# Two 512-column units in the input projection of an encoder layer, in place of four of 256

## The chip, the cores and the metric

The kernel runs on one core of a Trainium2 chip. The metric is the device time of one execution in microseconds (us); several executions are timed and their median is given. A profile of one execution shows what each engine did: TensorE (PE in the profile, with its weight loads as PEld), VectorE (DVE), ScalarE (ACT), GpSimd (POOL) and SyncE (SP), whose queue issues nearly all DMA transfers.

## The reference

One encoder layer with one set of weights is applied to 1024 prompt tokens and 256 sample tokens (1280 in all; attention does not cross between the two groups). Everything is float32, the model width is 1024.

```python
n = _rms_norm(h, g_mix, NORM_EPS)
z = jnp.einsum('bsd,dc->bsc', n, w_in).astype(f32)      # w_in: 1024 x 2304
# columns: A queries 512, A keys 512, A values 512, B queries 512, B keys 128, B values 128
qa, ka, va, qb, kb, vb = jnp.split(z, cuts, axis=-1)
...
oa = _diff_attention(qa, ka, va, lam, _alibi_slopes())  # mixer A: 4 heads, two softmax maps each
oa = _rms_norm(oa, g_subln, SUBLN_EPS) * (1.0 - lam_init)
...
qb = _rms_norm(qb.reshape(bsz, s_len, B_HEADS, HEAD_DIM), g_qnorm, NORM_EPS)   # mixer B: 8 query heads
kb = _rms_norm(kb.reshape(bsz, s_len, B_KV_HEADS, HEAD_DIM), g_knorm, NORM_EPS)
qb = _axial_rope(qb, ang_r, ang_c).reshape(bsz, s_len, B_KV_HEADS, B_GROUP, HEAD_DIM)
kb = _axial_rope(kb, ang_r, ang_c)
ob = _gqa_attention(qb, kb, vb).reshape(bsz, s_len, B_WIDTH)
h = h + jnp.einsum('bsc,cd->bsd', jnp.concatenate([oa, ob], axis=-1), w_out)
a = jax.nn.relu(jnp.einsum('bsd,df->bsf', _rms_norm(h, g_mlp, NORM_EPS), w_ff1))
h = h + jnp.einsum('bsf,fd->bsd', a * a, w_ff2)
gate = jax.nn.sigmoid(jnp.einsum('bsd,de->bse', _rms_norm(h, g_ple, NORM_EPS), w_ple_gate))
h = h + gate * jnp.einsum('bsp,pd->bsd', p_l, w_ple_proj)
return _rms_norm(h, g_final, NORM_EPS)
```

## The kernel before

**Numbers.** A float32 operand is split into a high part (rounded to the matmul's input format F32R) and a low part, the rest. A product is three matmuls: high x high, high x low, low x high. `load_w` (L162) does this for weights: a DMA into a staging buffer `raw`, a copy on ScalarE to the high part `wh` (L175), a subtraction to the low part `wl` (L176) on VectorE, or on GpSimd for the narrow A units. `load_x` (L247) does it for x, scaled by the gain, and fills `xh` and `xl`, which stay in SBUF.

**The in-projection.** Tokens come in 10 tiles of 128. Eight blocks of 128 model channels times three products make 24 matmuls for a tile and a unit of columns (`tok_pairs` L264, `mm_gen` L237). The units of columns are:

- `b_unit(2)`: mixer B's keys and values, 256 columns; `va_unit(0)`: values of A's heads 0 and 1, 256 columns. They run in alternation while x is still being loaded: `hook` starts the loads of x and of its row statistics (`stats_x` L256) for the later tokens.
- `b_unit(0)`: four of mixer B's query heads, 256 columns, woven with `va_unit(1)`, values of A's heads 2 and 3.
- `b_unit(1)`: the other four query heads, woven with `qk_a(0)`: keys, then queries of A's head 0, here with the weights stationary and up to 512 tokens as columns (`qk_unit` L372).

`weave` (L214) lets a side generator emit matmuls in proportion to the estimated time of the main one. The weights of the 256-column units share one ring of `WHB` = 11 buffers (each for high and low) and `RAWB` = 6 staging buffers. `load` (L90) chains the input DMAs, so that they are issued in the order of the program on the SP queue.

A `b_unit` tile is followed by `norm_rope` (L278): squares of the psum bank on ScalarE (L283), a scaled copy (L284), the sum per head (L287), a reciprocal root in small operations (L135 to 149), the rotation on GpSimd and VectorE (L292 to 299), and the product with the root (L301). Two tiles later TensorE transposes the result pair of heads by pair (L323). When a chunk of up to 512 tokens is transposed, `finish` (L311) splits it into high and low parts and stores it to DRAM (`qd`, `kd`). A `va_unit` tile is scaled, split (L367, L368) and stored (`vad`, L370). `R` (L444) holds the row statistics of all tokens, transposed by a TensorE instruction into `rp` (L439) and spread over the partitions by way of DRAM; `qk_unit` needs it in L382.

**Attention** reads keys, queries and values back from DRAM. Its rounds are planned by hand: each unit's scores, maxima, exponentials, transposes and value products are put into numbered rounds, and a side generator fills in the A heads 1 to 3 of the in-projection (`qk_rest`), then the output projection. Before round 0 it runs filler of an estimated 14 us (`PRE`). Its tiles take the SBUF that the in-projection's pool `bp` gives back; only two slots, `Q0` and `Q1`, exist from the start, and hold the first keys and queries of mixer B.

The order within each engine comes from a scheduler that simulates the program in time when it is built: among instructions that are ready in that simulation the earlier one in the program goes first, so matmuls of a later tile can stand ahead of those of an earlier one. That order is then fixed. PSUM has eight banks: two for `pj` (`psv`, `psa`), two for `pb` (`psb`), two each for the transposes `tr0` and `tr1` (B's key and value unit also uses `tr1` for two tiles).

The main loop of the first stage and the weave of the others:

```python
gens = [b_unit(2, w_kv, hook), va_unit(0, w_va0)]
for n in range(NT // 2):
    for g in gens:
        for _ in itertools.islice(g, 8):
            pass
...
weave(b_unit(0, w_b0), va_unit(1, w_va1), 1.0)
weave(b_unit(1, wload(1792, dma=load)), qk_a(0), 1.0)
```

## Time and profile before

| what | value |
| --- | --- |
| median of 3 runs | 1715.35 us (1713.63 to 1719.48) |
| the profiled execution | 1713.47 us, span 1711.7 us, granted TensorE clock 0.996 |
| TensorE busy | 1669.0 us, 98% of the span |
| VectorE, ScalarE, GpSimd busy | 69%, 50%, 40% |
| in-projection, up to the last query matmul | to about 183 us |
| first attention scores | 197.4 us |

The span is the part of an execution that the profile shows. Matmuls overlap, so a matmul's own duration is longer than the distance between two of them; the distance is what they cost. "Idle before" is the time for which an engine had nothing, and the name behind the arrow is what ended it.

### The profile page before, as it was taken

The page shows a single profiled execution, that of the slowest core. Times are in us where ns is not written, and L with a number is a line of the kernel's source. Part 1 is how long each engine was busy: PE and PEld are TensorE (multiplying, and loading weights), DVE is VectorE, ACT ScalarE, POOL GpSimd, SP SyncE. Part 2 cuts the span into 40 slices and gives each one's busy share as a digit, 9 for nine tenths or more (in the row PEclk, how much of TensorE's full clock was granted, in tenths as well). Part 3 has the DMA queues.
Part 4 walks back from the last instruction along what each step waited for, and adds up shares of the span by engine and source line. Part 5 has one row for each costly group of instructions (what it writes and reads, how often), then busy time and mean ns, then how long its engine had stood idle before and what let it go on. Part 6 is the DMA issues. An engine that isn't in the chain of part 4 may idle for free.

```text
span 1711.7 us, 27194 instructions
## 1 busy us (share of the span) xinstructions
PE 1669.0 (98%) x9849; PEld 1488.7 (87%) x9849; DVE 1182.8 (69%) x2110; ACT 861.9 (50%) x1731; POOL 691.6 (40%) x671
## 2 busy tenths in 40 slices
...
GB/s 314 271 90 115 202 169 124 141 88 105 273 155 113 165 81 111 150 219 103 158 154 121 132 144 136 128 213 360 198 217 200 129 206 192 167 120 67 35 44 50
DMA packets 187835, 263.60 MB, mean 154 GB/s; under 512 B 13226, under 2 KB 120628, under 8 KB 187700
## 3 DMA queue, kind: packets, MB, share of 16 engines
...
## 4 chain that ended last, share of the span: by engine, by line
PE 81%; DVE 6%; DMA 4%; ACT 3%; issue 3%; POOL 2%; SPq 1%; POOLq 0%; DVEq 0%; ACTq 0%
PE psa L240 6%; PE sc L573 5%; PE pso L240 5%; PE av L651 5%; PE psg L156 4%; PE tr L627 4%; PE psb L240 3%; PE psv L240 2%; DMA xt<-in_x 1%; PE psp L156 1%; DVE pl L638 1%; PE f__14851 L156 1%; PE f__16240 L156 1%; PE f__15200 L156 1%; PE f__16582 L156 1%
## 5 line engine op out<-in xcount | busy, mean ns | idle before, releaser
L1299 ACT ACTIVATE ao<-ar 128x1280 fp32r<-128x1280 f32 x56 | 71.3, 1275 | 193.9 <-PE f__16244 L156 37.9
L573 PE MATMUL sc<-kt,qt 128*128 128x512 f32 (+1 forms) x576 | 156.8, 392 | 7.1 <-ACT p L598 4.7
L638 DVE TENSOR_TENSOR pl<-tr,ph 128x512 fp32r<-128x512 f32 x204 | 137.9, 684 | 32.3 <-ACT ph L633 30.9
L1301 DVE TENSOR_TENSOR ao<-ar,ao 128x1280 fp32r<-128x1280 f32 x56 | 87.7, 1567 | 100.3 <-ACT ao L1299 100.3
L633 ACT ACTIVATE ph<-tr 128x512 fp32r<-128x512 f32 x204 | 119.8, 596 | 57.6 <-PE tr L627 51.2
L1012 POOL TENSOR_SCALAR w1r<-w1r,gmlp 128x256 f32<-128x256 f32 x128 | 98.8, 790 | 68.2 <-DMA w1r<-in_w_ff 45.8
L240 PE MATMUL pso<-ow,mt 128*128 128x512 f32 x480 | 119.6, 395 | 2.9 <-DVE osq L678 1.3
L627 PE MATMUL tr<-ident,p 128*128 128x128 f32 x768 | 116.0, 274 | 6.4 <-DVE pl L638 5.7
L573 PEld LDWEIGHTS sc<-kt,qt 128*128 128x128 f32 x576 | 99.3, 189 | 25.2 <-ACT p L598 6.3
L156 PE MATMUL psg<-gw,n 128*128 128x512 f32 (+1 forms) x504 | 115.4, 384 | 0.0
L627 PEld LDWEIGHTS tr<-ident,p 128*128 128x128 f32 x768 | 91.7, 141 | 23.1 <-DVE pl L638 9.3
L156 PEld LDWEIGHTS psg<-gw,n 128*128 128x128 f32 x504 | 90.8, 188 | 19.5
L1087 ACT ACTIVATE w<-w1s 128x512 fp32r<-128x512 f32 x64 | 40.0, 628 | 133.5 <-POOL w1s L1094 64.2
L240 PEld LDWEIGHTS pso<-ow,mt 128*128 128x128 f32 x480 | 87.6, 189 | 20.9 <-DVE osq L678 2.0
L651 PE MATMUL av<-ph,vt 128*128 128x256 f32 x544 | 102.4, 289 | 1.0 <-DVE osq L678 0.4
L612 POOL TENSOR_SCALAR p<-p,rl 128x1024 f32<-128x1024 f32 x64 | 75.2, 1176 | 50.5 <-DVE rl L610 45.4
L590 DVE TENSOR_REDUCE mm<-sc 128x1 f32<-128x1024 f32 (+1 forms) x80 | 84.2, 1055 | 9.5 <-PE sc L573 9.1
L651 PE MATMUL av<-pl,vt 128*128 128x256 f32 x408 | 89.9, 302 | 0.0
L651 PEld LDWEIGHTS av<-ph,vt 128*128 128x128 f32 x544 | 82.3, 190 | 6.5 <-ACT ph L633 0.9
L598 ACT ACTIVATE p<-sc,mm 128x1024 f32<-128x1024 f32 x64 | 71.3, 1115 | 24.8 <-DVE mm L590 18.5
L586 DVE CUSTOM_DVE_ANT_0 p<-sc,dist 128x1024 f32<-128x1024 f32 x64 | 77.6, 1218 | 8.0 <-PE sc L573 4.4
L595 ACT ACTIVATE p<-p,mm 128x1024 f32<-128x1024 f32 x64 | 73.5, 1149 | 18.4 <-DVE mm L586 17.6
...
## 6 DMA issues: line engine op xcount, KB each, us to landing
...
```

The costliest lines, as they stand in the source:

```text
L156: PE.matmul(ps, a, b, start=start and i == 0, stop=stop and i == n - 1)
L240: PE.matmul(ps, a, b, start=i == 0, stop=i == n - 1)
L573: PE.matmul(ps[:, h0:h0 + n], shared["q"][:, cc, v, i * P:(i + 1) * P], kt[:, s0 + h0:s0 + h0 + n], start=v == 0, stop=v == 1)
L586: V.tensor_tensor_reduce(out=p[:, :sn], in0=ps[:, :sn], in1=dst_t[:, off:off + sn], scale=SLOPES[idx], scalar=3.0e38, op0=ALU.add, op1=ALU ...
L590: V.tensor_reduce(out=st["m", i][:, 0:1], in_=ps[:, :sn], axis=AX.X, op=ALU.max, negate=True)
L612: G.tensor_scalar(p[:, :sn], p[:, :sn], rl[:, 0:1], 1.0, op0=ALU.mult, op1=ALU.mult)
L627: PE.transpose(t[:, jj, i * P:(i + 1) * P], st["ws"][i][:, j * P:(j + 1) * P], ident)
L633: S.activation(ph, st["tr", j2], AF.Copy)
L638: V.tensor_tensor(pl, st["tr", j2], f(st["ph", j2][:]), op=ALU.subtract)
L651: PE.matmul(st["av"][:, :256], x_, y_, start=j2 == 0 and n == 0, stop=j2 == nj - 1 and n == len(pr) - 1)
L1012: G.tensor_scalar(raw[:, k], raw[:, k], gmlp[:, 4 * kh + k:4 * kh + k + 1], 1.0, op0=ALU.mult, op1=ALU.mult)
L1301: V.tensor_tensor(ao[:, 1], a, f(ao[:, 0]), op=ALU.subtract)
```

## The change

B's eight query heads become one unit of 512 columns (`b_unit(False, w_b)`), and A's values for all four heads become one (`va_unit(w_va)`, in the first stage beside B's keys and values). The unit of two kinds of 256 columns in the middle is gone. Head 0's keys and queries (`qk0`) start on their own once the first stage is done, for an estimated 9 us (`QLEAD`), and are then woven into the query unit at a ratio of 0.4 (`QRATIO`).

- A block of 512-column weights is one of 128 channels instead of two; the number of loads stays at 20 for these units. The ring has 10 buffers (`WHB`), staging has 4 (`RAWB`); the first two blocks of B's key and value weights go into the slots `Q0` and `Q1`.
- `norm_rope` works on eight heads at once. Of its buffers, `sq`, `ra` and `rb` are single instead of double.
- The queries are transposed and stored in chunks of 256 tokens, two pairs of heads in a PSUM bank.
- A's value tile is evacuated in two halves of 256 columns; the buffers `vl` are 3 instead of 2.

```diff
--- before.py
+++ after.py
@@ -156,24 +156,33 @@
             PE.matmul(ps, a, b, start=start and i == 0, stop=stop and i == n - 1)
 
     w_dma = []
-    WHB = 11
-    RAWB = 6
-
-    def load_w(src, cols, n, rawp, wp, tag, lo_eng, between={}, dma=dma):
+    WHB = 10
+    RBB = 1
+    VLB = 3
+    QLEAD = 9000.0
+    QRATIO = 0.4
+    RAWB = 4
+
+    def load_w(src, cols, n, rawp, wp, tag, lo_eng, between={}, dma=dma, own=False):
 
         c0 = cols
         hi, lo = [], []
         kn = 512 // n
-        kw = {"bufs": WHB} if n == 256 else {}
+        kw = {"bufs": WHB} if n >= 256 else {}
         for kk in range(KD // kn):
             if kk in between:
                 between[kk]()
-            raw = rawp.tile([P, kn, n], F32, tag="raw", name=f"raw{tag}", bufs=RAWB if n == 256 else 2)
+            raw = rawp.tile([P, kn, n], F32, tag="raw", name=f"raw{tag}", bufs=RAWB if n >= 256 else 2)
             w_dma[:] = [dma(raw, src[kk * kn * P:(kk + 1) * kn * P, c0:c0 + n].rearrange("(k p) c -> p k c", p=P))]
-            a = wp.tile([P, kn, n], F32R, tag="wh", name=f"wh{tag}", **kw)
-            b = wp.tile([P, kn, n], F32R, tag="wl", name=f"wl{tag}", **kw)
+            if own and kk < 2:
+
+                ab = slot(f"Q{kk}", [P, 2, kn, n], F32R, f"wo{tag}")
+                a, b = ab[:, 0], ab[:, 1]
+            else:
+                a = wp.tile([P, kn, n], F32R, tag="wh", name=f"wh{tag}", **kw)[:]
+                b = wp.tile([P, kn, n], F32R, tag="wl", name=f"wl{tag}", **kw)[:]
             S.activation(a, raw, AF.Copy)
-            lo_eng.tensor_tensor(b, raw, f(a[:]), op=ALU.subtract)
+            lo_eng.tensor_tensor(b, raw, f(a), op=ALU.subtract)
             hi += [a[:, i, :] for i in range(kn)]
             lo += [b[:, i, :] for i in range(kn)]
         return hi, lo
@@ -277,18 +286,18 @@
 
     def norm_rope(ps, t, nh, g):
         r1 = rstd1[:, t:t + 1]
-        sq = bp.tile([P, 4, 64], F32, tag="sq", name="sq")
-        zg = bp.tile([P, 4, 64], F32, tag="zg", name="zg")
+        sq = bp.tile([P, 8, 64], F32, tag="sq", name="sq", bufs=1)
+        zg = bp.tile([P, 8, 64], F32, tag="zg", name="zg")
         ps3 = ps[:, :nh * 64].rearrange("p (h d) -> p h d", d=64)
         S.activation(sq[:, :nh], ps3, AF.Square, scale=r1)
         V.scalar_tensor_tensor(zg[:, :nh], ps3, r1, g[:, None, :].to_broadcast([P, nh, 64]),
                                op0=ALU.mult, op1=ALU.mult)
-        ss = bp.tile([P, 4], F32, tag="ss", name="ss")
+        ss = bp.tile([P, 8], F32, tag="ss", name="ss")
         V.tensor_reduce(out=ss[:, :nh], in_=sq[:, :nh], axis=AX.X, op=ALU.add)
-        rr = bp.tile([P, 4], F32, tag="rr", name="rr")
+        rr = bp.tile([P, 8], F32, tag="rr", name="rr")
         rsqrt(rr[:, :nh], ss[:, :nh], 1.0 / 64, 1e-6, bp, nh, f"rq{nh}")
-        a = bp.tile([P, 4, 64], F32, tag="ra", name="ra")
-        b = bp.tile([P, 4, 64], F32, tag="rb", name="rb")
+        a = bp.tile([P, 8, 64], F32, tag="ra", name="ra", bufs=RBB)
+        b = bp.tile([P, 8, 64], F32, tag="rb", name="rb", bufs=1)
         G.tensor_tensor(a[:, :nh], zg[:, :nh], rc[:, t:t + 1, :].to_broadcast([P, nh, 64]), op=ALU.mult)
         z4 = zg[:, :nh].rearrange("p h (a b e) -> p h a b e", a=2, b=2)
         b4 = b[:, :nh].rearrange("p h (a b e) -> p h a b e", a=2, b=2)
@@ -297,34 +306,41 @@
             V.tensor_tensor(b4[:, :, :, q, :], z4[:, :, :, 1 - q, :],
                             s4[:, None, :, q, :].to_broadcast([P, nh, 2, 16]), op=ALU.mult)
         G.tensor_tensor(a[:, :nh], a[:, :nh], b[:, :nh], op=ALU.add)
-        o = bp.tile([P, 4, 64], F32, tag="ro", name="ro", bufs=3)
+        o = bp.tile([P, 8, 64], F32, tag="ro", name="ro", bufs=3)
         V.tensor_tensor(o[:, :nh], a[:, :nh], rr[:, :nh, None].to_broadcast([P, nh, 64]), op=ALU.mult)
         return o.rearrange("p h d -> p (h d)")
 
-    def b_unit(u, w, hook=None):
-
-        kv = u == 2
-        npair = 1 if kv else 2
+    def b_unit(kv, w, hook=None):
+
+        npair = 1 if kv else 4
         pend = collections.deque()
         pss = {}
 
         def finish(c0, cn, trp):
-            for m in range(npair):
-                hl = (bp.tile([P, 2, 512], F32R, tag="qkl", name="qkl", bufs=1) if kv
-                      else bp.tile([P, 2, 512], F32R, tag="xr", name="qkl", bufs=2))
-                S.activation(hl[:, 0, :cn], trp[m][:, :cn], AF.Copy)
-                V.tensor_tensor(hl[:, 1, :cn], trp[m][:, :cn], f(hl[:, 0, :cn]), op=ALU.subtract)
-                dst = kd[4] if kv else qd[4 + 2 * u + m]
-                dma(dst[:, :, c0:c0 + cn].rearrange("v p t -> p v t"), f(hl[:, :, :cn]))
+
+            if kv:
+                hl = bp.tile([P, 2, 512], F32R, tag="qkl", name="qkl", bufs=1)
+                S.activation(hl[:, 0, :cn], trp[0][:, :cn], AF.Copy)
+                V.tensor_tensor(hl[:, 1, :cn], trp[0][:, :cn], f(hl[:, 0, :cn]), op=ALU.subtract)
+                dma(kd[4][:, :, c0:c0 + cn].rearrange("v p t -> p v t"), f(hl[:, :, :cn]))
+                return
+            for m in range(2):
+                hl = bp.tile([P, 2, 2, 256], F32R, tag="xr", name="qkl", bufs=2)
+                tr = trp[m].rearrange("p (a t) -> p a t", a=2)
+                S.activation(hl[:, 0], tr, AF.Copy)
+                V.tensor_tensor(hl[:, 1], tr, f(hl[:, 0]), op=ALU.subtract)
+                for a in range(2):
+                    dma(qd[4 + 2 * m + a][:, :, c0:c0 + cn].rearrange("v p t -> p v t"), f(hl[:, :, a]))
 
         def tr(args):
             o, t, c0, cn, trp = args
             for m in range(npair):
-                PE.transpose(trp[m][:, t * P - c0:t * P - c0 + P], o[:, m * P:(m + 1) * P], ident)
+                q = t * P - c0 + m % 2 * 256
+                PE.transpose(trp[m // 2][:, q:q + P], o[:, m * P:(m + 1) * P], ident)
             if (t + 1) * P == c0 + cn:
                 finish(c0, cn, trp)
 
-        for (c0, cn) in TCH:
+        for (c0, cn) in TCH if kv else [(c, 256) for c in range(0, T, 256)]:
             trp = None
             for t in range(c0 // P, (c0 + cn) // P):
                 if hook:
@@ -338,8 +354,8 @@
                         split3((ps, pss[1])[u_][:, :256], tok_pairs(w, u_)[6 * kq:6 * kq + 6], kq == 0, kq == 3)
                         yield 1.0
                 elif not kv or t != 1:
-                    yield from mm_gen(ps[:, :256], tok_pairs(w, t))
-                o = norm_rope(ps, t, 2 if kv else 4, gk if kv else gq)
+                    yield from mm_gen(ps[:, :256 if kv else 512], tok_pairs(w, t), 6 if kv else 3)
+                o = norm_rope(ps, t, 2 if kv else 8, gk if kv else gq)
                 if kv:
                     hl = bp.tile([P, 2, 2, 64], F32R, tag="vbl", name="vbl")
                     vps = ps[:, 128:256].rearrange("p (h d) -> p h d", d=64)
@@ -350,24 +366,25 @@
                     for j in range(2):
                         dma(vbd[j][t * P:(t + 1) * P, :], f(hl[:, j].rearrange("p v d -> p (v d)")))
                 if trp is None:
-                    trp = [pp1.tile([P, 512], F32, tag=f"tr{m}", name="trb", bufs=2) for m in range(npair)]
+                    trp = [pp1.tile([P, 512], F32, tag=f"tr{m}", name="trb", bufs=2) for m in range(1 if kv else 2)]
                 if len(pend) == 2:
                     tr(pend.popleft())
                 pend.append((o, t, c0, cn, trp))
         while pend:
             tr(pend.popleft())
 
-    def va_unit(u, w):
+    def va_unit(w):
         for t in range(NT):
             ps = pj("psv")
-            yield from mm_gen(ps[:, :256], tok_pairs(w, t))
-            hl = bp.tile([P, 2, 2, P], F32R, tag="vl", name="vl")
-            v3 = ps[:, :256].rearrange("p (h d) -> p h d", d=P)
+            yield from mm_gen(ps, tok_pairs(w, t))
             r1 = rstd1[:, t:t + 1]
-            S.activation(hl[:, :, 0, :], v3, AF.Copy, scale=r1)
-            V.scalar_tensor_tensor(hl[:, :, 1, :], v3, r1, f(hl[:, :, 0, :]), op0=ALU.mult, op1=ALU.subtract)
-            for j in range(2):
-                dma(vad[2 * u + j][t * P:(t + 1) * P], f(hl[:, j]))
+            for u in range(2):
+                hl = bp.tile([P, 2, 2, P], F32R, tag="vl", name="vl", bufs=VLB)
+                v3 = ps[:, u * 256:u * 256 + 256].rearrange("p (h d) -> p h d", d=P)
+                S.activation(hl[:, :, 0, :], v3, AF.Copy, scale=r1)
+                V.scalar_tensor_tensor(hl[:, :, 1, :], v3, r1, f(hl[:, :, 0, :]), op0=ALU.mult, op1=ALU.subtract)
+                for j in range(2):
+                    dma(vad[2 * u + j][t * P:(t + 1) * P], f(hl[:, j]))
 
     def qk_unit(dst, scale, w):
         wh, wl = w
@@ -384,19 +401,18 @@
             G.tensor_tensor(hl[:, 1, :cn], z, f(hl[:, 0, :cn]), op=ALU.subtract)
             dma(dst[:, :, c0:c0 + cn].rearrange("v p t -> p v t"), f(hl[:, :, :cn]))
 
-    def qk_a(h):
-
-        for c, dst, sc in ((512 + P * h, kd[h], 1.0), (P * h, qd[h], -0.125 / SLOPES[h])):
-            w = load_w(w_in, c, P, rawp, wp, "a", G, dma=load)
-            yield from qk_unit(dst, sc, w)
-
-    def wload(c, between={}, dma=dma):
-        return load_w(w_in, c, 256, bp, bp, "p", V, between, dma)
+    def qk_a(h, w):
+
+        yield from qk_unit(kd[h], 1.0, w)
+        yield from qk_unit(qd[h], -0.125 / SLOPES[h], load_w(w_in, P * h, P, rawp, wp, "a", G, dma=load))
+
+    def wload(c, n, between={}, dma=dma, own=False):
+        return load_w(w_in, c, n, bp, bp, "p", V, between, dma, own)
 
     first_x = functools.partial(load_x, 0, 256, dma=load)
-    w_kv = wload(2048, {1: lambda: first_x(4, 0, 2), 2: lambda: first_x(2, 4, 2, tag="xt"),
-                        3: lambda: first_x(2, 6, 2, tag="xt")}, load)
-    w_va0 = wload(1024, dma=load)
+    w_kv = wload(2048, 256, {1: lambda: first_x(4, 0, 2), 2: lambda: first_x(2, 4, 2, tag="xt"),
+                        3: lambda: first_x(2, 6, 2, tag="xt")}, load, True)
+    w_va = wload(1024, 512, dma=load)
     stats_x(0, 256, load)
     load_x(256, 256, dma=load)
     load(gk, g_kn.to_broadcast([P, 64]))
@@ -411,7 +427,7 @@
             stats_x(512 + P * t, 256, load)
 
 
-    gens = [b_unit(2, w_kv, hook), va_unit(0, w_va0)]
+    gens = [b_unit(True, w_kv, hook), va_unit(w_va)]
     for n in range(NT // 2):
         for g in gens:
             for _ in itertools.islice(g, 8):
@@ -419,14 +435,15 @@
     for g in gens:
         drain(g)
 
-    w_b0, w_va1 = wload(1536, dma=load), wload(1280, dma=load)
+    qk0 = qk_a(0, load_w(w_in, 512, P, rawp, wp, "a", G, dma=load))
+    w_b = wload(1536, 512, dma=load)
     gple = col("gple", g_ple, KD)
     load(gmlp, g_mlp)
     gsub = col("gsub", g_subln, 1)
     S.activation(gsub, gsub, AF.Copy, scale=1.0 - LAM_INIT)
     lam_t = bp.tile([P, D], F32, tag="xt", name="lam_t", bufs=2)[:, :256].rearrange("p (a b) -> p a b", a=4)
     load(lam_t.rearrange("p a b -> p (a b)"), lams.to_broadcast([P, 256]))
-    lam_p = bp.tile([P, 4, 64], F32, tag="sq", name="lam_p")[:, :2]
+    lam_p = bp.tile([P, 8, 64], F32, tag="sq", name="lam_p", bufs=1)[:, :2]
     V.tensor_tensor(lam_p, lam_t[:, 0::2, :], lam_t[:, 1::2, :], op=ALU.mult)
     lam_e = bp.tile([P, 2], F32, name="lam_e", bufs=1)
     V.tensor_reduce(out=lam_e, in_=lam_p, axis=AX.X, op=ALU.add)
@@ -437,14 +454,16 @@
 
     rp = pp1.tile([P, 512], F32, tag="pb", name="rp", bufs=2)
     PE.transpose(rp[:NT, :P], rstd1, ident)
-    rr_t = bp.tile([P, 4, 64], F32, tag="sq", name="rr_t").rearrange("p h d -> p (h d)")[:NT, :P]
+    rr_t = bp.tile([P, 8, 64], F32, tag="sq", name="rr_t", bufs=1).rearrange("p h d -> p (h d)")[:NT, :P]
     S.activation(rr_t, rp[:NT, :P], AF.Copy)
     rd = dp.tile([1, T], F32, name="rd")
     dma(rd.rearrange("a (t p) -> (a t) p", p=P), rr_t)
     dma(R, rd.to_broadcast([P, T]))
 
-    weave(b_unit(0, w_b0), va_unit(1, w_va1), 1.0)
-    weave(b_unit(1, wload(1792, dma=load)), qk_a(0), 1.0)
+    lead = 0.0
+    while lead < QLEAD:
+        lead += next(qk0)
+    weave(b_unit(False, w_b), qk0, QRATIO)
     bs.close()
```

## The prediction

> **What bounds the kernel now.** I read the page first, then busy time by stretch, then the waits of TensorE, then the chain of waits, and last the start of the kernel engine by engine.
>
> ```profile
> PE 1669.0 (98%) x9849; PEld 1488.7 (87%) x9849; DVE 1182.8 (69%) x2110; ACT 861.9 (50%) x1731; POOL 691.6 (40%) x671
> ```
>
> TensorE is busy 98% of the span, so only three things can move the time: fewer microseconds of streamed columns, fewer waits of TensorE, or new ones. Busy time by stretch (each pair is busy us and instruction count, for PE, PEld, DVE, ACT, POOL; then clock, DMA share, GB/s):
>
> ```profile
> 5.00:67.00 62.00, 60.53 (x494) 59.37 (x495) 50.62 (x198) 49.28 (x139) 10.61 (x20) 1.00 0.94 310
> 67.00:125.00 58.00, 58.00 (x499) 58.00 (x499) 40.88 (x118) 19.18 (x52) 17.21 (x22) 1.00 0.48 148
> 125.00:183.00 58.00, 58.00 (x403) 53.40 (x401) 40.69 (x112) 15.79 (x45) 24.26 (x28) 1.00 0.28 99
> 183.00:260.00 77.00, 76.24 (x447) 66.32 (x445) 54.17 (x101) 46.06 (x91) 40.40 (x38) 1.00 0.72 199
> 260.00:560.00 300.00, 287.67 (x1807) 250.99 (x1806) 241.72 (x449) 213.77 (x439) 159.51 (x170) 0.99 0.50 145
> ```
>
> The in-projection is the first three rows. TensorE has no idle time from 67 to 183 us, although DVE is busy only 40.88 of 58 us there. The DMA engines are full (0.94) in the first row and half idle afterwards. All the waits of TensorE in the first 190 us (total us, times, longest):
>
> ```profile
> PE psb L156 <- ACT xh L252: 5.2, 1, 5.2
> PE psb L240 <- DVE vbl L348: 0.7, 1, 0.7
> PE psb L156 <- ACT whp L175: 0.4, 1, 0.4
> ```
>
> The 5.2 us is the first load of x, which stays. So the stage is a queue of matmuls with nothing between them, and the change must be costed by the matmuls.
>
> **The change, part by part.**
>
> *Matmuls.* Each 512-column unit replaces two of 256: 2 x 10 tiles x 24 = 480 matmuls of 512 columns stand for 960 of 256. Streamed columns are the same; weight loads halve. The pace is in the chain of waits (start, duration, what):
>
> ```profile
> 73.19 0.70 PE psv L240 x6
> ...
> 75.99 0.70 PE psv L240 x6
> ...
> 125.65 0.69 PE psa L240 x3
> 126.34 0.71 PE psb L240 x6
> ...
> 184.15 7.54 PE psa L240 x33
> ```
>
> From 73.19 to 75.99 four pieces of six 256-column matmuls ran: 2.80 / 24 = 0.1167 us each, 0.2333 a pair. One of 512 takes 0.69 / 3 = 0.230 us mixed with 256-wide ones and 7.54 / 33 = 0.2285 in a run. Gain per pair 3.3 to 4.8 ns, times 480: 1.6 to 2.3 us. Most new matmuls follow others of 512, so I take 2.3. The Trainium skill, page "TensorE: Matmul & The Clock Gate", section "Back-to-back issue gap", gives a warm gap of N/2.4 + 2.5 ns; by it a pair would save one 2.5 ns overhead, an estimate of 480 x 2.5 = 1.2 us instead of 2.3. The trace agrees on the direction, not on the size: its overheads are larger.
>
> *VectorE, ScalarE, GpSimd.* The norm and rotation run 10 times on 512 columns instead of 20 times on 256. Before (mean ns is the second number after the bar):
>
> ```profile
> L761 DVE SCALAR_TENSOR_TENSOR zl<-psa,R 128x512 f32<-128x512 f32 x12 | 8.3, 691 | 9.4 <-PE psa L240 7.4 <-issue 1.7 <-POOL p L612 0.2
> L284 DVE SCALAR_TENSOR_TENSOR zg<-psb,rstd,gq 128x256 f32<-128x256 f32 x20 | 9.7, 483 | 21.1 <-ACT sq L283 21.1
> L297 DVE TENSOR_TENSOR rb<-zg,cs 128x128 f32<-128x128 f32 x40 | 18.9, 511 | 0.0
> L301 DVE TENSOR_TENSOR ro<-ra,rr 128x256 f32<-128x256 f32 x20 | 8.5, 426 | 2.4 <-DVE rr L149 0.5
> ```
>
> By these, one 512-wide pass of zg or ro costs 0.69 instead of 2 x 0.48 or 2 x 0.43, and the two rb instructions between 2 x 0.51 and 4 x 0.51 against 4 x 0.51; the five small operations on the statistics are issued half as often. DVE thus saves one to two us a tile, 10 to 20 us in all, and none of it reaches the end, because TensorE covers it: 58.00 of 58. Were that cover gone, the tile interval of 24 x 0.2285 = 5.5 us would stand against about 6 us of DVE, half a microsecond a tile. That can happen only in the last two tiles, where head 0's queries and keys have run out (9 us of lead, then 0.4 of the rest, is used up at four fifths of the unit): 0 to 1 us, taken as 0, since the ring of two PSUM banks spans it.
>
> Value evacuations stay at 20 of 256 columns, value stores at 40, weight loads at 20 and their splits at 20, transposes at 40 for the queries: same work, nothing to pay. Query stores go from 12 to 20 smaller ones; eight more issues on the SP queue at about 0.4 us each are 3 us spread over some 80 us of stage, and the attention's loads behind them wait for the unit's end anyway. Taken as 0.
>
> *Between the phases.* The 0.7 us wait in the table above (transpose of the statistics, then the next unit's psum) should go, since head 0's keys now run at that place from their own pool, covering the splits of w_b: these can begin only as the value weights are released, but each release is 3 x 0.2285 = 0.69 us after the last and a split takes as long. Minus 0.7 (0 to 0.9 us).
>
> *The start.* This is what speaks against the change. Two MB of value weights instead of one must come before the second 256 tokens of x, through 4 staging buffers instead of 6, and the loads are chained in order.
>
> ```profile
> 4.33 5.29 SPq L93 DMA_DIRECT2D rawp<-in_w_in  x5
> ...
> 10.04 1.74 SPq L93 DMA_DIRECT2D xt<-in_x  x2
> 11.82 0.98 SPq L93 DMA_DIRECT2D xr<-in_xT  x2
> ```
> ```profile
> 4.33 0.69 DVE L176 TENSOR_TENSOR wlp<-rawp,whp 128x512 fp32r<-128x512 f32 x1 [3.31 <-ACT whp L175]
> ...
> 8.53 0.69 DVE L176 TENSOR_TENSOR wlp<-rawp,whp 128x512 fp32r<-128x512 f32 x1
> ...
> 9.93 0.69 DVE L176 TENSOR_TENSOR wlp<-rawp,whp 128x512 fp32r<-128x512 f32 x1
> ...
> 11.32 3.23 DVE L176 TENSOR_TENSOR wlp<-rawp,whp 128x512 fp32r<-128x512 f32 x5
> ```
> ```profile
> L175 ACT ACTIVATE whp<-rawp x8: 614/630/634, 3.7 to 13.2; 128x512 fp32r<-128x512 f32 x8
> ...
> DMA to landing us min/median/max: 2.9/5.6/6.4
> ```
> ```profile
> 7.06 0.41 PE L156 MATMUL psb<-whp,xh 128*128 128x256 f32 x1
> 7.28 0.41 PE L156 MATMUL psb<-wlp,xh 128*128 128x256 f32 x1
> ...
> 12.18 0.40 PE L240 MATMUL psv<-whp,xh 128*128 128x256 f32 x2
> 12.41 0.28 PE L156 MATMUL psb<-wlp,xh 128*128 128x256 f32 x1
> ...
> 18.95 0.28 PE L240 MATMUL psb<-whp,xh 128*128 128x256 f32 x1
> ```
>
> A staging buffer is free when DVE has written the low part: the first four at 5.0, 9.2, 10.6 and 12.0 us. A lap of the ring is landing plus copy plus subtraction: 2.9 + 0.63 + 0.69 = 4.2 us at the best row, 6.9 at the median. So the eight value blocks are ready, at 4.2, at about 11 (behind the others), 13.4, 14.8, 16.2, 15.5, 17.6, 19.0, 20.4; at 6.9, at 11.9, 16.1, 17.5, 18.9, 18.8, 23.0, 24.4, 25.8. TensorE is free for values at about 12 us and two tiles take 48 x 0.2285 = 11 us, to 23. If it takes both tiles block by block, it ends 6 x 0.2285 = 1.4 us after the last block: 21.8 (no wait) or 27.2 (4.2 us late). The next x loads are issued behind the eighth weight load and two xt loads, at some 18 to 21 instead of 11.8; in the trace it is 18.95 - 11.82 = 7.1 us from there to the first matmul on those tokens, so 25 to 28: 1 to 2 us more. The sum is 0 to 5 us; fewer transfers in flight make landings shorter than the median, so I take 2.0, nearer the fast lap. After that each 256 tokens give TensorE 2 x 24 x (0.1167 + 0.2285) = 16.6 us against 11.2 before, and the DMA engines fall behind no more.
>
> *Into attention.*
>
> ```profile
> 184.15 7.54 PE psa L240 x33
> 191.68 0.22 PE trb L323 x2
> 191.90 5.62 PE psa L240 x36
> 197.52 0.70 PE sc L573 x3
> ```
>
> After the last projection matmuls TensorE already works 13 us on head 1's keys while the last norm, transposes and stores finish. With eight heads that tail is longer by wider passes (0.2 to 0.6 us each in some six of them, two more evacuations): 3 to 4 us, inside the 5.6 us after the transposes. Taken as 0; without that cover it costs its full 3 to 4.
>
> Sum: -2.3 - 0.7 + 2.0 = -1.0 us against the profiled execution's own 1713.47 us (span 1711.7): 1712.5. The runs' median, 1715.35, lies 1.9 higher, so I say 1714.4 for a median. With the bounds it is 1713.47 - 3.2 to 1713.47 - 1.6 + 5 + 1 = 1710.3 to 1717.9, in medians about 1712 to 1720.
>
> **Rivals.**
>
> *The attention moves too (faster).* TensorE idles 12.3 us between 260 and 560 us (300 - 287.67), in many short waits:
>
> ```profile
> PE tr L627 <- DVE pl L638: 3.6, 6, 1.1
> PE sc L573 <- ACT p L598: 2.7, 4, 1.6
> ```
>
> A different order of filler work there could remove a third of the 12.3. With no stall at the start that gives -3.0 - 4.1 = -7.1: 1706.4, in medians 1708. For it: head 0's keys are ready earlier and DVE has less backlog as the stage ends. Against it: the attention's order is not edited, and between 183 and 260 only 0.8 us is idle.
>
> *The start starves (slower).* If the PE queue holds tile 0's 24 value matmuls wholly before tile 1's, tile 0 ends 0.7 us after the last block, at 26.5 by the slow lap, and tile 1 at 32.0: 9 us late. A long gap may also drop the clock: matmuls at 7.06 and 7.28 are 0.22 us apart, twice 0.1167, and that phase lasted some 4 us, so a return costs about 2. The Trainium skill, same page, section "What's actually happening", has the clock fall back after an idle window of about 3.4 us; no run here shows a return. Together 9 + 2 - 3.0 = +8: 1721.5, in medians 1723. For it: the full DMA share, 0.94. Against: at 12.18 us the queue put value matmuls between two others, so its order fills gaps. It decides once the stall passes 8 us.
>
> *Weight loads set the pace (much faster).* Then a 512-column matmul would cost what one of 256 does, and 480 x 0.1167 = 56 us would go: 1657. The run of 33 at 0.2285 speaks against it. The skill's section "Back-to-back issue gap" has 131 ns for N = 512 as a sustained figure, by which 480 x (0.2333 - 0.131) = 49 us would go, an estimate; the trace contradicts it.
>
> *It does nothing that shows* is nearly my forecast: the terms are -3.2 to +5 us.
>
> **How the numbers follow.** Three runs spread from 1713.63 to 1719.48, so 0.3%, 5.1 us, is about what a measurement can tell from no change: faster is below 1710.2, slower above 1720.5. Forecast (terms cancel) 0.53; attention gains or all good bounds together 0.26; weight loads 0.01; starved start, or the same waits of attention growing, 0.20. The forecast's own range is 1710 to 1720. To leave out no more than two in ten I reach to both side cases, 1704 to 1724.
>
> **What the profile after would show.** 512-wide psb and psv at 0.2285 to 0.230 us each; value matmuls at 12 to 27 us with a wait on the value weights' copy or subtraction of 0 to 5 us; no wait on vbl between the phases; DVE busy 10 to 20 us less up to the first score matmul, for nothing; first scores within 3 us of 197. I am wrong if that first score comes over 5 us earlier or later, or if idle time between 260 and 800 us changes by more than 4.

## The result and the profile after

The change makes the kernel slower by about 7 us: 1722.16 us (median of 7 runs, 1720.43 to 1724.21) against 1714.94 for the kernel before on the same chip (7 runs, 1712.49 to 1719.48). The ratio is 1.0042, with a 95% interval of 1.0031 to 1.0052. The prediction said 1714.4. The measured time lies near the price of its rival of a starved start (1723), but that is luck: none of that rival's waits appears. The profiled execution took 1720.43 us, span 1718.0, against 1713.47 and 1711.7.

The page of after, the counterpart of the first line in the prediction:

```profile
PE 1669.6 (97%) x9369; PEld 1466.6 (85%) x9369; DVE 1168.7 (68%) x2008; ACT 856.0 (50%) x1699; POOL 686.6 (40%) x651
```

TensorE has 480 matmuls fewer and is as busy as before (1669.0). VectorE is busy 14.1 us less, as forecast (10 to 20), for nothing. So all but 0.6 us of the 6.3 us by which the span is longer are idle time of TensorE. By stretch (busy us and count for PE, PEld, DVE, ACT, POOL; then clock, DMA share, GB/s), after:

```profile
5.00:67.00 62.00, 61.89 (x350) 54.31 (x351) 45.73 (x162) 46.30 (x123) 9.38 (x16) 1.00 0.93 312
67.00:125.00 58.00, 58.00 (x289) 48.32 (x288) 31.07 (x82) 18.75 (x47) 16.42 (x17) 1.00 0.50 153
125.00:183.00 58.00, 58.00 (x280) 47.65 (x279) 42.96 (x85) 14.94 (x35) 24.81 (x20) 1.00 0.28 96
183.00:260.00 77.00, 72.64 (x421) 62.67 (x420) 52.61 (x95) 42.53 (x84) 36.34 (x34) 1.00 0.71 195
260.00:560.00 300.00, 285.93 (x1807) 249.04 (x1806) 240.62 (x446) 213.46 (x440) 156.62 (x168) 1.00 0.49 142
```

The in-projection (first three rows) is as full as before. The loss begins in the fourth: 77 - 72.64 = 4.4 us idle where before had 0.8. What TensorE waited for in the first 260 us of after (total us, times, longest):

```profile
PE psb L156 <- ACT xh L261: 5.0, 1, 5.0
PE sc L592 <- DMA qt<-qd: 1.9, 1, 1.9
PE av L670 <- ACT ph L652: 1.4, 1, 1.4
PE psa L249 <- DVE o L718: 0.6, 1, 0.6
PE tr L646 <- DVE pl L657: 0.4, 1, 0.4
```

The first wait was there before (5.2). The second and third are new, and both lie in the attention's first units. Farther on there is another new one, at the start of the MLP (waits from 640 to 880 us, after and then before; the numbers behind `f__` differ by 742 between the kernels, so f__9782 in after is f__10524 in before):

```profile
PE f__9782 L156 <- DVE nlo L1140: 2.1, 1, 2.1
PE f__9653 L156 <- ACT nhi L1139: 2.1, 1, 2.1
...
PE f__9707 L156 <- DVE nlo L1140: 1.2, 1, 1.2
```
```profile
PE f__10395 L156 <- ACT nhi L1120: 2.7, 1, 2.7
...
PE f__10449 L156 <- DVE nlo L1121: 1.2, 1, 1.2
...
PE f__10524 L156 <- DVE q L1213: 0.3, 1, 0.3
```

The new wait is the 2.1 us of f__9782 on `nlo`, the low part of the normalised activations; the other two have their counterparts before.

To see where lost time stays lost, I compared the start of the same instruction in each trace with its start in the first trace of before. The first column is the first matmul of head 1's keys (`whq`, the filler that follows the in-projection; 183.0 us in before); the others are medians over the ScalarE and VectorE instructions within 20 us from the given time. Positive is later, in us.

```
kernel                              filler    240    400    520    700    780    880
before, second run                    -0.2   -0.2   -0.2   -1.3   -1.4   -1.5   -1.6
after                                 -2.0    2.5    2.8    3.7    3.5    4.4    6.5
after, second run                     -1.8    3.9    4.3    4.6    4.5    4.9    5.7
before_late_table                      0.4    0.4    0.5    0.3    0.4    0.7    0.2
before_order_of_after                  1.2    1.4    1.4    1.9    2.0    2.1    4.4
before_other_mlp_order                 4.0    4.0    4.0    4.1    4.0    4.6    4.7
after_order_of_before                 -1.8    0.6    0.6    1.2    0.8    1.7    4.0
after_order_of_before_same_queue      -2.8    0.0    0.1   -0.5    1.3    1.6    3.8
the same, second run                  -2.3    1.8    1.9    0.8    0.9    2.2    3.1
after_head_weights_on_scalar_queue    -2.7    2.6    2.5    3.5    3.0    4.3    5.2
after_order_and_scalar_queue          -2.3    1.0    0.9   -0.6    0.9    2.2    3.0
queries_narrow                        -5.7    7.1    7.3    9.3    8.9    9.5    9.5
after_halved_matmuls                   1.2    7.0    7.2    5.6    5.4    6.1    6.7
```

The in-projection of after ends 2 us earlier, as its terms said (-1.0 was forecast). By 240 us that is gone and 2.5 us more with it; another 2 us go at the start of the MLP, between 780 and 880. The second run of after is after_more_filler_1000, and that of after_order_of_before_same_queue is after_order_and_filler_500: both came out with the same instructions in the same order (below). Such pairs differ by up to 1.8 us in a column.

Much of that difference is the granted TensorE clock. In every trace it falls to half one to four times before the end, for 3.4 us (a few times 6.8), which costs up to 1.7 us. All but one of these falls begin during a wait of TensorE of 1.0 to 3.3 us or within some 2 us behind it, but the same wait has one in one trace and none in another. After and then its second run, from 215 to 219 us and from 792 to 797 us (the clock is the third number from the end):

```profile
215.00:219.00 4.00, 4.00 (x32) 3.83 (x31) 3.42 (x6) 2.48 (x5) 0.07 (x1) 1.00 1.11 288
792.00:797.00 5.00, 3.86 (x21) 3.86 (x22) 5.00 (x10) 3.03 (x6) 3.01 (x4) 0.66 0.00 0
```
```profile
215.00:219.00 4.00, 4.00 (x20) 3.89 (x19) 2.07 (x4) 1.37 (x3) 0.34 (x1) 0.57 1.11 268
792.00:797.00 5.00, 3.42 (x27) 3.42 (x28) 5.00 (x10) 3.15 (x7) 3.45 (x5) 1.00 0.02 3
```

TensorE is fully busy from 215 to 219 us in both, but does 32 matmuls in one and 20 in the other. Between 183 and 260 us this fall comes in the second runs of after and of after_order_of_before_same_queue, in after_head_weights_on_scalar_queue, queries_narrow, after_halved_matmuls and after_other_mlp_order, and in no trace of before or its variants.

### The profile page after: what moved, and what is told of

Read it like the earlier page. It is cut to its first block, busy times and chain, and to the rows that moved or that the text cites. A ratio compares the mean times of both kernels' runs of the same rounds, so it can differ in the third digit from the quotient of the medians.

```text
span 1718.0 us, 26081 instructions
## 1 busy us (share of the span) xinstructions
PE 1669.6 (97%) x9369; PEld 1466.6 (85%) x9369; DVE 1168.7 (68%) x2008; ACT 856.0 (50%) x1699; POOL 686.6 (40%) x651
## 4 chain that ended last, share of the span: by engine, by line
PE 80%; DVE 8%; issue 4%; POOL 3%; ACT 3%; DMA 2%; SPq 1%; POOLq 0%; DVEq 0%; ACTq 0%
PE sc L592 5%; PE av L670 5%; PE psa L249 5%; PE psb L249 4%; PE psg L156 4%; PE pso L249 4%; PE tr L646 4%; PE psv L249 3%; PE psp L156 1%; DVE pl L657 1%; DVE nlo L1140 1%; DVE mm L609 1%; DVE p L605 1%; PE f__15498 L156 1%; PE f__14458 L156 1%
```

## The experiments

Before stands for runs of the kernel before on the same chip in each comparison. One more profile of before alone (before_again, one run) took 1712.37 us; it gives the first row above:

> The kernel before, unchanged, for a second profile. It tells which steps between the two traces are the kernel's and which are chance. If the steps of 0.9 us at 450, 1.1 us at 730 and 2.1 us at 800 to 860 us are chance, this trace is apart from the first one of before by as much there; if they belong to the changed kernel, this trace lies within 0.3 us of the first one throughout.

The second trace leaves the first by 1.1 us between 400 and 520 us and moves against it by at most 0.2 from column to column elsewhere, so a single step of about 1 us can be chance.

**Is a matmul of 512 columns cheaper than two of 256?** after_halved_matmuls issues each 512-column tile of values and queries as 24 matmuls of 256 columns and then 24 more (the line of the values; that of the queries is alike):

```diff
-            yield from mm_gen(ps, tok_pairs(w, t))
+            # the first 256 columns, 24 pairs, then the last 256
+            yield from mm_cut(ps, tok_pairs(w, t), 12)
```

> After with each value and query tile's 24 matmuls of 512 columns issued as 24 of the first 256 columns and then 24 of the last 256, in the same bank; units, loads, evacuations and the orders up to the attention's first units stay those of after, the MLP's start comes out near before's order. My prediction's term 'a matmul of 512 columns costs 0.2285 instead of 2 x 0.1167' says that the in-projection gets 2.3 us longer. Rival 'a matmul whose weights change every time costs the same per column at both widths': within 0.6 us, the last query matmul at 180.0 to 181.0 instead of 182.5. In the total the MLP's order takes about 2.5 off in both: 1.0042 by the first, 1.0028 by the rival.

Measured: 1723.21 (1.0054, 1.0041 to 1.0068). The chain of waits gives two value tiles at a place without a wait, first in after, then here (start, duration, what):

```profile
65.10 11.19 PE psv L249 x48
```
```profile
66.23 11.20 PE psv L261 x96
```

48 matmuls of 512 columns take 11.19 us, 0.2331 each; 96 of 256 take 11.20. Nothing is saved per column while the weights are the moving operand. For the stage as a whole neither side's number came: the last query matmul ended 3.3 us later (183.85 against 180.59), where the prediction's term asked for 2.3 and the rival for less than 0.6. Of this, 1.6 us is a wait for head 0's evacuation, which after does not have:

```profile
PE psa L249 <- DVE zl L408: 1.6, 1, 1.6
```

Another 1.5 us lie in the values (57.49 us start to start, against 55.97 in after): between 15 and 20 us, while the first tile's weights still arrive, some of their matmuls come 0.22 to 0.50 us apart instead of 0.117. The clean stretch has neither, so its pace per column stands.

**The values alone.** queries_narrow keeps the 512-column value unit and puts the queries back into two units of four heads (one line of several):

```diff
-    weave(b_unit(False, w_b), qk0, QRATIO)
+    weave(itertools.chain(b_unit(0, w_b0), b_unit(1, w_b1)), qk0, QRATIO)
```

> The changed kernel with half of the change undone: the queries go back to two units of four heads, 256 columns each, woven one after the other with head 0's queries and keys at the same ratio; the values stay at 512 columns. Tail theory (the last tile's eight-head norm, its two large evacuations and four stores stand in the SP queue ahead of attention's first loads, so TensorE waits some 4 us between 205 and 229 us): the loads start at most 14 us after the last query matmul instead of 17.5, and 3 to 4 us come back: 1718 to 1719 against 1722. Rival (it is the order of filler around it, with head 0's keys and queries used up before the last query tiles, that hurts): 1722, since that order stays.

Measured: 1719.21 (1.0034, 1.0023 to 1.0046). Most of the loss (1.0034 of 1.0042) is there without the eight-head unit, again chiefly between the filler's first matmul and 240 us. (The traced execution, 1722.69, is the slowest of its six, so the table's row is above the median.) So the width of the last norm is not what makes most of it.

**The staging buffers.** before_other_mlp_order is before with four staging buffers instead of six, after's number; its order at the start of the MLP changes too.

```diff
-    RAWB = 6
+    RAWB = 4
```

> The kernel before with 4 instead of 6 staging buffers for the wide weights. In the instruction lists attention's first units keep the order of before on ScalarE, VectorE and SP; the start of the MLP takes another order on ScalarE and VectorE, the one that the trace with narrow queries had. Order theory: 2 to 2.5 us more waits of TensorE between 780 and 830 us, none more between 205 and 245: 1716 against 1714. Rival (the step at 800 us is passed down from earlier lateness): no step. The staging theory of my prediction's start, up to 5 us late with 4 buffers in place of 6, would show as waits before 40 us.

Measured: 1715.9 (1.0012, 1.0004 to 1.0021), and all of it is lost in the first 180 us: the table's row stays at 4.0 from the filler on. Its waits of TensorE up to 183 us:

```profile
PE psb L156 <- ACT xh L252: 4.9, 1, 4.9
PE psv L240 <- DVE vl L368: 2.3, 1, 2.3
PE psb L240 <- ACT xh L252: 0.7, 1, 0.7
```

So the kernel with four staging buffers is about 4 us late while the values are 256 wide, but not at the start: the wait on `vl` ends at 68.89 us. VectorE had stood 2.47 us, up to 65.95, before the low part of a weight block of the next unit, with the evacuation of `vl` behind it, and from 68.9 to 72.3 us the granted clock is 0.50, another 1.7 us. In after no such wait appears behind the first x; that twice the value work per token tile covers the loads is argued, not tested.

**The order in the attention's first units.** Each engine's order is fixed when the program is built, and it changed where nothing was edited. On ScalarE, after and then before (start, us, instruction, idle before and its releaser):

```profile
226.50 0.63 ACT L756 ACTIVATE whq<-rawq 128x512 fp32r<-128x512 f32 x1 [2.85 <-DMA rawq<-in_w_in]
227.03 1.13 ACT L614 ACTIVATE p<-p,mm 128x1024 f32<-128x1024 f32 x1
```
```profile
223.25 1.15 ACT L595 ACTIVATE p<-p,mm 128x1024 f32<-128x1024 f32 x1
...
224.81 0.63 ACT L737 ACTIVATE whq<-rawq 128x512 fp32r<-128x512 f32 x1 [0.33 <-DMA rawq<-in_w_in]
```

In after the split of the filler's weights stands before an exponential that could have run, and ScalarE sits 2.85 us until the weights land; TensorE's 1.4 us wait on `ph` follows from it. Three kernels test the order. after_order_of_before gives head 0's work out more slowly, and SyncE's order changes in part; after_order_of_before_same_queue keeps SyncE's order in these units and all orders of the MLP as they are in after; those of ScalarE, VectorE and with them TensorE become before's (head 0's own place beside the queries, from 105 us on, changes in both):

```diff
-    QRATIO = 0.4
+    QRATIO = 0.3     # after_order_of_before; 0.32 in ..._same_queue
```

> The changed kernel with the weave ratio 0.3 instead of 0.4. In the instruction lists ScalarE and VectorE get, over attention's first units, exactly the order of before (exponentials ahead of the weight split), SP's list still differs, and the start of the MLP stays in the changed kernel's order. Order theory: of the 4 us more between 205 and 245 us about 2 come back (ScalarE no longer stands 2.9 us before an exponential waiting for a filler's weights): 1720 against 1722. Rival (late loads): the wait only moves to another instruction, 1722.

> After with QRATIO 0.32: SyncE's order and the MLP's start are after's, only ScalarE's and VectorE's order in the attention's first units is before's (the exponential ahead of the filler's weight split). Theory 'order': the wait of av on ph (1.4 us) goes and 225 to 245 us falls from 2.3 to about 0.9; with the loads still near 197 the wait on qt stays, 205 to 225 us 2.3. Ratio about 1.0030. Rival 'loads only': 205 to 245 us stays at 4.6, ratio 1.0042.

before_order_of_after does the opposite: before with PRE 15000 instead of 14000, by which its TensorE, ScalarE and VectorE run these units in after's order.

> The kernel before, its in-projection untouched, with 15 us instead of 14 us of estimated filler ahead of attention's first round. In the instruction lists this gives ScalarE and VectorE, over attention's first units, exactly the order of the changed kernel (a weight split of the filler stands ahead of a unit's exponentials, twice), while SP's list there stays that of before; the start of the MLP is ordered nearly as in the changed kernel too. Order theory (the changed in-projection made the build's scheduler choose other orders downstream, and these cost): TensorE waits 1.5 to 2 us more between 205 and 245 us and 2 us more between 780 and 830: 1717 to 1718 against 1714. Rival (the orders are harmless by themselves; what costs is that the loads come late in SP's queue): 1714.

Measured: 1717.05 (1.0022, 1.0013 to 1.003); 1718.39 (1.0028, 1.002 to 1.0037); 1717.58 (1.0021, 1.0012 to 1.003). In the second the exponential runs first again, and the wait on `ph` is 0.3 us. About a third of the loss goes, though the intervals of 1.0028 and of after's 1.0042 (1.0037 in its second run) overlap. The traces say the same: from the filler to 240 us the four with after's order lose 4.5 to 5.7 us (after, its second run, after_head_weights_on_scalar_queue and loads_past_filler, which goes from -1.1 to 4.1), the four with before's order 2.4 to 4.1, and where the clock doesn't fall it is 4.5 and 5.2 against 2.4 to 3.3. But in before the same order costs nothing at that place (1.2 at the filler, before any changed instruction, and 1.4 at 240): the weights had landed there when the split came up. So the order hurts only where the transfers are late for it. The total of before_order_of_after was forecast at 1717 to 1718 for a loss here and one at the MLP; only the second came (below), so that the number was hit in part by chance.

A further kernel, meant to put 0.7 us more filler ahead of the first scores (PRE 14500), came out with the same instructions in the same order as after_order_of_before_same_queue, so it is a repeat: 1718.68 (1.0028, 1.0016 to 1.004), wait on `qt` 1.9. Its expectation was not tested:

> QRATIO 0.32 (1.0028, with before's order of ScalarE and VectorE in the attention's first units) and PRE 14500: three more of the filler's matmuls (0.7 us) ahead of the first scores. Theory 'TensorE early, loads not': the 1.7 us wait on qt becomes about 1.0 and the ratio 1.0024. Rival: unchanged, 1.0028 or more.

**The wait of the scores on their queries.** The loads into the attention were issued 4 us later in after (table of distances at 197.91 instead of 193.65). SyncE's queue of after:

```profile
193.55 2.10 SPq L333 DMA_DIRECT2D qd<-qkl  x4
196.24 0.36 SPq L783 DMA_DIRECT2D kd<-zl  x1
197.49 0.37 SPq L747 DMA_DIRECT2D rawq<-in_w_in  x1
197.91 0.56 SPq L970 DMA_DIRECT2D dist<-in_dist  x1
```

I first tried what stands ahead of them on the queue. before_late_table holds the table back in before until head 1's second key tile is stored; after_head_weights_on_scalar_queue moves `rawq` to ScalarE's queue, after_order_and_scalar_queue does that at QRATIO 0.32, loads_past_filler puts the second `rawq` pair and the stores of head 1's keys on GpSimd's.

```diff
-    dma(dst_t, dist)                                              # before_late_table
...
+    with tc.issue_after(<store of head 1's second key tile>):
+        dma(dst_t, dist)
...
-            dma(raw, w_in[...])                                   # rawq
+            S.dma_start(raw, w_in[...])                           # the two on ScalarE's queue
```

> Before with one transfer held back: the load of the distance table is issued after the store of head 1's second key tile, behind which it stands in after, instead of before it, and one weight load and two key loads of the same queue stand behind it with it. All other orders, the MLP's too, are before's. Its issue moves from 193.65 to about 198. Theory 'late loads alone cost the attention's first units what they cost in after': idle time from 205 to 245 us rises from 0.7 to 3 to 4.6, ratio 1.0013 to 1.0025. Rival 'a late load costs only where the order of ScalarE and VectorE is after's too': under 1 us, ratio within 1.0007.

> After with the loads of the filler's weights (rawq) issued by ScalarE's queue instead of SyncE's, so that the distance table no longer stands behind one of them (1.25 us: 196.24 to 197.49). The order of arithmetic on ScalarE and VectorE and the MLP's start are after's. Theory 'the loads are late because of what is queued before them': the table is issued about 196.5, 1.2 us earlier, the wait of the scores on qt (1.9 us) becomes 0 to 0.7, ratio 1.0033 to 1.0037. Rival 'what counts is the order on ScalarE, where the split of those weights stands before the exponentials': the split still waits for its load at 226, 225 to 245 us keeps 2.3 of idle time, ratio 1.0042 or more.

> QRATIO 0.32 and the filler's weights on ScalarE's queue together. If late loads and order are the two halves of the loss in the attention's first units, 205 to 245 us idles 1 to 2 us and the ratio is about 1.0018 (what is left is the MLP's start, 2.3 us, less the shorter in-projection). If neither is, 1.0040.

> The changed kernel with the three stores of head 1's keys and the two staging loads after them issued on GpSimd's queue instead of SP's, so that attention's first loads do not stand behind them in SP's queue; ScalarE and VectorE keep the changed kernel's order. Late-load theory: the distance load is issued right behind the last tile's four stores, at about 195.7 instead of 197.9, the 1.9 us wait of the scores on qt goes, and 2 us come back: 1720 against 1722. Order theory: nothing or little, 1722.

Measured: 1714.12 (1.0007, 0.9998 to 1.0016), with the table issued at 198.35, later than in after, and no wait on `qt`; 1719.62 (1.0035, 1.0023 to 1.0046), with the table at 195.96 and the wait grown to 2.7 (here ScalarE stands only 0.3 us before the split and the wait on `ph` is gone, but the clock falls behind the wait on `qt`); 1718.79 (1.003, 1.0018 to 1.0042), wait 2.7; 1721.99 (1.0045, 1.0032 to 1.0058), where the table did not come earlier (198.83, in a trace that is 0.9 us later than after's from the filler on), so that it does not test the queue. The place of the table on the queue is not the cause. But before_late_table delays the table alone, by 4.7 us; the values and keys behind it kept their time, so it does not say what the lateness of all of them costs.

Next the amount of filler. qk_to_the_end (QRATIO 0.2) leaves head 0's work to the end, behind the queries; more_filler (PRE 18000) gives TensorE more filler ahead of the first scores:

> The changed kernel with the weave ratio 0.2 instead of 0.4, so that some 7 us of head 0's queries remain behind the last query tile as cover for its tail. Tail theory: the query unit ends 7 us earlier, attention's first loads are issued at about 191 instead of 198 us, and the 3 to 4 us between 205 and 229 come back: 1718 to 1719 against 1722. Rival (the wait has its cause inside attention's own order): 1722.

> The changed kernel with 18 us instead of 14 us of estimated filler (head 1's keys and queries) ahead of attention's first round. Tail theory: the first scores come 4 us later, the loads are there by then, TensorE waits under 1 us between 205 and 235; some of the gain may be lost later, where filler is then missing: 1718 to 1721. Rival (the wait is inside attention's order): no wait goes, 1722 or slower.

Measured: 1723.83 (1.0054, 1.0041 to 1.0067) and 1732.42 (1.0113, 1.0098 to 1.0129). In the first the table is issued at 187.4, ten us earlier, and the waits on `qt` and `ph` are gone; waits on `p` and `mm` take their place (3.0 and 1.2 us by 300 us), and by 400 us it is 4.5 us late in the measure of the table; the 3 to 4 us that were expected back did not come. In the second the wait on `qt` is gone too, with 136 filler matmuls ahead of those scores instead of 120, and the filler is missing later: TensorE is idle 15.0 us from 260 to 480 where after is idle 9.5 (220 - 204.97 and 220 - 210.52):

```profile
260.00:480.00 220.00, 204.97 (x1286) 178.83 (x1285) 171.57 (x310) 152.52 (x313) 120.77 (x126) 0.98 0.49 142
```
```profile
260.00:480.00 220.00, 210.52 (x1342) 184.06 (x1341) 176.13 (x326) 159.52 (x329) 126.56 (x134) 1.00 0.52 150
```

PRE 15000 was to do a little of the same. It came out with after's instructions in after's order on every engine, and so is a repeat of after: 1720.6 (1.0037, 1.0025 to 1.005).

> After with PRE 15000 instead of 14000: TensorE gets six more of the filler's 512-column matmuls (1.4 us of work that it does later otherwise) ahead of the attention's first scores. The orders of ScalarE, VectorE, SyncE and the MLP's start are after's. Theory 'the in-projection's gain is given back because TensorE arrives 2 us earlier at scores whose loads are not earlier': the 1.9 us wait of the scores on qt shrinks to about 0.5, 205 to 225 us from 2.3 to about 0.9, and the ratio comes to about 1.0034 if the filler isn't missed later. Rival 'the loads are late because the queue is': the wait stays at 1.5 or more. If the filler is missed later, 225 to 480 us idles 1.4 more and the ratio stays at 1.0042.

Then what holds the loads? The last rotated queries (`ro`) are written on VectorE, and TensorE transposes them into `trb`; in after

```profile
187.18 0.69 DVE L310 TENSOR_TENSOR ro<-ra,rr 128x512 f32<-128x512 f32 x1
...
192.83 0.69 DVE L331 TENSOR_TENSOR qkl<-trb,qkl 128x512 fp32r<-128x512 f32 x1 [4.36 <-ACT qkl L330]
193.44 0.68 DVE L780 SCALAR_TENSOR_TENSOR zl<-psa,R 128x512 f32<-128x512 f32 x1
194.04 0.68 DVE L331 TENSOR_TENSOR qkl<-trb,qkl 128x512 fp32r<-128x512 f32 x1
```
```profile
191.79 0.60 PE L339 MATMUL trb<-ident,ro 128*128 128x128 f32 x4
```

and in before

```profile
187.92 0.43 DVE L301 TENSOR_TENSOR ro<-ra,rr 128x256 f32<-128x256 f32 x1
```
```profile
191.52 0.38 PE L323 MATMUL trb<-ident,ro 128*128 128x128 f32 x2
```

The queries are ready at 187.9 in after, half a microsecond earlier than before, and wait 3.9 us for the transposes: TensorE's order is fixed, and 45 filler matmuls stand ahead of these in after, 36 in before (counted in the traces). Nine more at 0.2285 us are 2.06 us, the whole gain of the in-projection. So the chain from the transposes through the split, the stores and the loads is not earlier, and with two 512-wide splits and another evacuation between them the last query store goes 2 us later. From there the DMA engines are the limit (190 to 197 and 197 to 214 us, before, then after; the DMA share is the number before the last):

```profile
190.00:197.00 7.00, 7.00 (x43) 6.18 (x42) 1.45 (x3) 2.33 (x5) 2.11 (x2) 1.00 0.90 308
197.00:214.00 17.00, 17.00 (x83) 14.05 (x82) 8.27 (x13) 7.37 (x14) 8.38 (x8) 1.00 1.08 278
```
```profile
190.00:197.00 7.00, 7.00 (x46) 6.29 (x45) 2.31 (x4) 3.18 (x6) 2.64 (x3) 1.00 0.60 216
197.00:214.00 17.00, 15.06 (x70) 12.11 (x69) 7.97 (x12) 6.90 (x12) 8.36 (x9) 1.00 1.03 271
```

They are full from 197 on in both, but start later in after (0.60 instead of 0.90). TensorE has 120 filler matmuls up to the third group of scores in either kernel; having begun them 2 us earlier it runs out of them, and the scores begin when they did before, at 213.47 against 212.93:

```profile
213.47 1.16 PE L592 MATMUL sc<-kt,qt 128*128 128x512 f32 x4 [1.94 <-DMA qt<-qd]
```
```profile
212.93 1.09 PE L573 MATMUL sc<-kt,qt 128*128 128x512 f32 x4
```

That is read from the traces; no kernel with the transposes ahead of the filler was run. The nearest one, after_order_of_before, says that an earlier transpose alone does not do it. There 39 filler matmuls stand ahead, and the last transposes come 1.45 us earlier than in before, yet the last query store is issued at 194.41 (193.15 in before), the table at 196.01, and the same scores wait again:

```profile
190.07 0.60 PE L339 MATMUL trb<-ident,ro 128*128 128x128 f32 x4
```
```profile
212.82 1.16 PE L592 MATMUL sc<-kt,qt 128*128 128x512 f32 x4 [1.63 <-ACT zl L781]
```

(The profile names `zl`, but a load of `qt` lands at 212.73.) So the wider splits and the four stores behind the transposes count too, and how the lateness divides between them is open. What the runs show is that the wait goes when there is more filler (more_filler) or the queries end earlier (qk_to_the_end), and that the queue's head does not decide it.

One kernel took the eight query stores of the last 256 tokens to GpSimd's queue (at QRATIO 0.3 and LATE 156, the pair of the next part):

```diff
-                    dma(qd[4 + 2 * m + a]...)
+                    (G.dma_start if c0 >= 1024 else dma)(qd[4 + 2 * m + a]...)
```

> As after_both_orders (QRATIO 0.3, LATE 156), and the eight query stores of the last 256 tokens are issued on the GpSimd queue instead of SyncE's, so that the attention's loads are queued behind fewer stores. Theory 'the loads are late because they stand behind the queries' last stores': the distance table lands its issue 1.5 to 3 us earlier than 195.9, the wait of the first scores on it or on a DMA goes and the total is 1 to 2 us under after_both_orders: 1.0000 of before. Rival 'they are bound by the last key stores of the filler, which stand there too': the distance table is issued within 1 us of 195.9 and the total stays; GpSimd waiting for VectorE's query parts may then cost 1 us, up to 1.0013.

Measured: 1722.85 (1.005, 1.0038 to 1.0063); the table issued at 196.16, against 195.73 in after_both_orders, unmoved, as the rival said.

**The start of the MLP.** Its order on VectorE and ScalarE, too, differs between before and after, and before_order_of_after, in which the in-projection is untouched, has nearly after's. It also has after's wait there:

```profile
PE f__10524 L156 <- DVE nlo L1121: 2.1, 1, 2.1
```

Ten traces have after's order there or nearly so: both of after, the four at QRATIO 0.3 and 0.32, after_head_weights_on_scalar_queue, loads_past_filler, before_order_of_after and qk_to_the_end. Nine have this 2.1 us wait behind one of 1.2 on f__9707 (f__10449), and in loads_past_filler the same two are 1.1 and 2.2. They lose 0.8 to 3.5 us from 780 to 880 us (3.0 - 2.2 in the table to 7.3 - 3.8 in loads_past_filler). The spread is the clock: in the four where it stays at 1.00 behind these waits they lose 0.8 or 0.9, in the five where a fall of 3.4 us begins there, between 790 and 794.3 us, 2.1 to 2.3, and in loads_past_filler, with one of 6.8 us, 3.5. Before, before_late_table, before_other_mlp_order, queries_narrow and after_halved_matmuls have 0.7 us of the wait or none and no fall of the clock at that place, and lose -0.5 to 0.6. So the order there costs some 0.8 us by its waits, and 1.4 more where the clock falls behind them. To take it out of after I changed the round from which filler is given out faster, alone and with QRATIO 0.3:

```diff
-    LATE = 160
+    LATE = 156
```

> After with one constant of the planner changed (LATE 160 to 156: from which round on the filler is given out faster). The orders of ScalarE, VectorE and SyncE through the in-projection and the attention's first units are those of after; the order of ScalarE and VectorE at the start of the MLP is nearer to before's. Theory 'the MLP order is a loss of its own': TensorE's idle time from 640 to 830 us falls from 21.8 to about 19.2 and its 2.1 us wait on VectorE's nlo there goes; the total is 2 to 3 us under after, about 1.0027 of before; 205 to 245 us stays at 4.6. Rival 'the MLP only hands on a late attention': the idle time there stays at 21 to 22 and the ratio at 1.0042.

> After with QRATIO 0.3 (head 0's work given out more slowly beside the queries, with which the attention's first units run in before's order) and LATE 156 (another order at the start of the MLP). Theory 'the parts add': 205 to 245 us idles about 3.2 as with QRATIO 0.3 alone, 640 to 830 about 19.3 instead of 21.9; the total is 2.5 us under that of QRATIO 0.3 alone (1.0022), so 1.0007 of before (0.9997 to 1.0017). Rival 'they are the same loss seen at two places': 1.0020 or more.

Measured: 1723.44 (1.0052, 1.0039 to 1.0065) and 1720.77 (1.0041, 1.0029 to 1.0054): both worse, not better by 2.5 us. From 780 to 880 they lose only 0.2 and 0.1 us (lateness 10.9 to 11.1 and 6.9 to 7.0), so the loss there did go, although waits of 1.5 and 0.7 us on the same f__9782 stay; but between 520 and 700 us, where the constant gives the filler out faster, they lose 6.8 and 4.2 us (3.5 to 10.3, 1.6 to 5.8) and after nothing. No run changes that order without this.

No version beat before. The best of after's variants is after_order_of_before, at 1.0022.

## Why the prediction was wrong, by its own steps

**What bounds the kernel** held: TensorE, and its idle time is the result.

**Matmuls (-2.3)** was mis-sized. Both ends of the bound came from rows of `psa`, where the weights are stationary and tokens are the moving columns; 0.2285 does not carry over to `psv` and `psb`. They take 0.2331, and two of 256 take 0.2333: the term is near 0 in a clean stretch. Summed over the stage, with pieces broken up by other work in both kernels, the values went from 56.35 to 55.97 us, the queries with their transposes fell by about 0.7 and head 0's own matmuls by about 0.25 (sums of start to start; a few records are missing), about -1.3 in all. The Trainium skill, page "TensorE: Matmul & The Clock Gate", section "Back-to-back issue gap", has a fixed 2.5 ns a matmul, by which a pair would have saved that much; the clean stretch shows 0.2 ns, and its sustained 0.131 us for 512 columns was not seen here either.

**Between the phases (-0.7)** came out at -1.0: the transpose of the statistics was followed after 1.00 us before and 0.03 now.

**The start (+2.0)** came out at about 0.3, the rest of -2.0 beside the other terms: no wait on the value weights appears in after. Four buffers did make before late, by about 4 us, but at 66 to 72 us and through VectorE's queue and the clock, not through the late value blocks of the forecast.

**VectorE (0)** and **the last two tiles (0)** held. The wider passes are near their estimates (per pass `zg` 0.75, `ro` 0.69 against 0.69; each `rb` 0.82, between 0.51 and 1.02):

```profile
L306 DVE TENSOR_TENSOR rb<-zg,cs 128x256 f32<-128x256 f32 x20 | 15.6, 816 | 0.0
L293 DVE SCALAR_TENSOR_TENSOR zg<-psb,rstd,gq 128x512 f32<-128x512 f32 x10 | 7.5, 751 | 13.1 <-ACT sq L292 13.1
L310 DVE TENSOR_TENSOR ro<-ra,rr 128x512 f32<-128x512 f32 x10 | 6.9, 693 | 1.0
```

So the sum up to the filler, -1.0, was on the right side and small (-2.0 measured), with two errors against each other: 1.0 too much gain on the matmuls, 1.7 too much loss at the start.

**"Into attention ... taken as 0"** is the step that failed. It asked whether TensorE has work during the tail, and it has. It did not ask what the tail releases: the loads, which on full DMA engines set when the third group of scores can start. A TensorE that comes there 2 us earlier with the same 120 filler matmuls waits there (1.94 us). The step also says that the first scores come within 3 us of 197, which they do (198.5), so the check I named looked one place too early; the loss is between those and 240 us, 4.5 us from the filler on.

**"The attention's order is not edited"**, my argument against the first rival, is the second failure. The order did change, on ScalarE ahead of an exponential and 550 us farther on at the MLP, and both changes cost time. I had the mechanism as a gain or, in half a sentence, as "the same waits of attention growing", and priced no single case of it. The idle time from 260 to 560 us changed by 1.7 us (300 - 285.93 against 12.3), inside my bound; the MLP's start, which I never looked at, took 0.8 to 2.1.

**The clock** stood in the prediction only under the starved start, as a drop behind a long gap, priced at about 2 us, of which it said that no run showed it. The trace of before has two (0.50 from 446.0 to 449.4 and from 766.8 to 770.2 us), and the price was near (1.7). In after and its variants such falls also come behind waits of 1.8 to 3.3 us in the attention's first units and of 2.1 us at the MLP, and none at the start. The seven timed runs of after have a mean granted clock of 0.9949, the 78 of before that are on record with one (on five chips) 0.9961; 0.0012 of 1720 us is about 2 of the 7 us (an estimate).

In sum, on the profiled executions: -2.0 up to the filler, +4.5 to 240 us (some 1.6 of it for the order, since from the filler to 240 us two traces of after lose 5.1 on the mean and two of after_order_of_before_same_queue 3.5, in each pair one with a fall of the clock; the rest is the gain waiting for the loads, and some more that stays open), +0.3 to 400, +0.9 to 520, +0.7 to 780, +2.1 to 880 (some 1.3 of it the clock, by the second run's 0.8): +6.5 at 880 us, 6.3 in the span.
